# Matrix product with bias and residual: eight late residuals, another order of the first loads, a last store in more pieces

## The chip, the cores and the metric

The kernel runs on one core of a Trainium2 chip. The metric is the device time of one execution in microseconds (us), as the median of several runs. A core has five engines that run beside each other and meet only at semaphores: TensorE (PE in the profile; PEld is its loading of weights), VectorE (DVE), ScalarE (ACT), GpSimd (POOL) and SyncE (SP), which here only issues transfers. Transfers between the chip's main memory (HBM) and the on-chip memory run on 16 DMA engines. TensorE writes to PSUM, a small memory with 128 partitions, from which DVE reads here.

## The reference

```python
"x": np.random.randn(16, 512, 1024)         # float32
"weight": np.random.randn(1024, 768)
"bias": np.random.randn(768)
"residual": np.random.randn(16, 512, 768)

def reference(x, weight, bias, residual):
    return (np.matmul(x, weight) + bias + residual).astype(np.float32)
```

Flattened, x is 8192 rows of 1024, and the output and the residual are 8192 rows of 768. The kernel reads 33.6 MB of x, 25.2 MB of residual and 3.1 MB of weights, and writes 25.2 MB.

## The kernel before

**Tiles.** A tile is 128 rows of x. There are 64 tiles, in 8 super tiles of 8 (S = 0 to 7, so super tile 7 holds tiles 56 to 63). A transfer moves some of the tiles of one super tile: 4 KB per tile and partition for x, 3 KB for the residual and the output. In the table of transfers (`ORDER`), `('x', 1, 0, 4)` loads x of super tile 1, tiles 0 to 3 of it; `r` is the residual, `s` a store of the output, `w` a quarter of the weights, `b` the bias, and `c` a store of one column piece of the very last tile.

**A tile's way.** `cast` (L146, or halved L143 and L144) turns a tile of x into bf16. `transp` has TensorE transpose it, two bf16 values at a time as one 32-bit word (L154), and DVE copies the result to the chip's memory (L155). `mm` makes 16 matmuls (L161): four blocks of 256 in K, two halves of each, and 512 and 256 columns. The products of three tiles have room in PSUM (`PO`), the transposes of two (`PT`).

**Residual and bias.** For most tiles POOL adds the bias to the residual in place beforehand (L186), and DVE adds the product to that (L196); the result stands where the residual was and is stored from there. The first `EARLY_END` tiles go another way, since their residual lands late: DVE adds the product and the bias into a free buffer (L192; the buffer of residual 3, not yet loaded), and POOL adds that to the residual when it has come (L182). The residual of super tile 3 can be loaded only when all of these adds are done, and super tile 0 can be stored only then.

**Order of POOL's adds.** `pool_adds(upto)` goes through the list `ADDS` in its order, over tiles up to `upto`, and stops at the first one that can't be issued yet: its residual's load must have been issued, and for an early tile the DVE add too. It is called twice for each tile.

**Order of the transfers.** All transfers are issued by SP in the order of `ORDER`. `pump` issues, in the program's text, each one whose conditions are met: x into one of two buffers when the casts of its last user are written down, a residual into one of four buffers when the store from it is, a store when its tiles' sums are. At run time SP waits at each transfer until the instructions it depends on are done, and everything behind it in the list waits too. The weights' first landing place is the buffer of residual 1 (`w_st = R[1]`): piece S of the weights lies in its tiles 2S and 2S+1, and residual 1 can be loaded into a tile once the weight there has been cast. A transfer may name cuts of its partitions (`*cut`, `edges`), and is then issued in as many pieces.

**Head and tail.** `HEAD_ORDER` writes out the first tiles by hand: casts, transposes, weight casts (`wc`, L226), and matmuls of tiles 0 to 2 by quarters of K as the weights land. Then a loop runs over tiles 3 to 63: cast of tile t+2, POOL adds, transposes of t+1, matmuls of t, DVE's finish of t-1. The last tile's product is made in two column pieces, 512 and 256 (L255), each with its own DVE add (L259) and its own store.

Of the kernel before, what the change touches and what calls it, by code (L numbers as in the profile page):

```python
# [16 lines left out]
HEAD = 3  # L17
XT_N = 4
XB_N = 4
WARM = 12  # L20
EARLY_END = 6
TMP_SLOT = {0: 3}
ADDS = [6, 0, 7, 8, 1, 9, 2, 10, 3, 11, 4, 12, 5, 13, 14, 15]
HEAD_ORDER = [('cast', 0, 'v'), ('cast', 1, 's'), ('tr', 0), ('tr', 1), ('wc', 0, 0, 's'), ('wc', 0, 1, 'g'),
# [5 lines left out]
ORDER = [('x', 0, 0, 2), ('w', 0, 0, 2), ('x', 0, 2, 4), ('w', 1, 0, 2), ('b', 0, 0, 0), ('w', 2, 0, 2),  # L30
# [6 lines left out]


@with_exitstack
def kernel(  # L40
# [8 lines left out]
    nc = tc.nc  # L49
# [4 lines left out]
    N = weight.shape[1]  # L54
# [3 lines left out]
    chunks = [(0, 512), (512, N - 512)]  # L58
# [9 lines left out]
    def fixed(pool, name, n, shape, dt):  # L68
        return [pool.tile(shape, dt, name=f"{name}", tag=f"{name}{i}", bufs=1) for i in range(n)]
# [4 lines left out]
    XT = fixed(sb, "xt", XT_N, [P, n_q, P, 2], BF16)  # L74
    PO = fixed(ps, "psum_o", HEAD, [P, N], FP32)
# [7 lines left out]
    K_ = tc.keep_in_program_order  # L83
# [5 lines left out]
    def pump():  # L89
        while queue:  # L90
            kind, S, j0, j1, *cut = queue[0]
            if kind == "c":
                need = [("outc", j1)]
            elif kind in ("w", "b"):
                need = []
            elif kind == "x":
                need = [("cast", J * (S - X_SLOTS) + j) for j in range(j0, j1)] if S >= X_SLOTS else []
            elif kind == "r":
                need = [("store", S - RO_SLOTS, j) for j in range(j0, j1)] if S >= RO_SLOTS else []
                if S == 1:  # L100
                    need = [("wcast", n_q - 1)]
                if S in TMP_SLOT.values():
                    need = [("add", t) for t in range(EARLY_END) if TMP_SLOT[t // J] == S]
            else:
                need = [("out", J * S + j) for j in range(j0, j1)]
            if not all(n in done for n in need):
                return
            queue.pop(0)
            if kind == "b":
                K_(nc.sync.dma_start(  # L110
                    out=bias_row.rearrange("(g p) n -> g p n", p=QUAD)[:, 0, :],
                    in_=bias[None, :].to_broadcast([P // QUAD, N]),
                ))
                continue
            if kind == "w":
                K_(nc.sync.dma_start(out=w_st[:, 2 * S + j0:2 * S + j1, :], in_=w_d[:, S, j0:j1, :]))  # L116
                continue
            if kind == "x":
                K_(nc.sync.dma_start(out=X[S % X_SLOTS][:, j0:j1, :], in_=x_d[S, :, j0:j1, :]))  # L119
            elif kind == "r":  # L120
                K_(nc.sync.dma_start(out=R[S % RO_SLOTS][:, j0:j1, :], in_=res_d[S, :, j0:j1, :]))
            else:
                n0, nl = (0, N) if kind == "s" else chunks[j1]
                j1 = j1 if kind == "s" else j0 + 1
                edges = [0, *cut, P]
                for p0, p1 in zip(edges, edges[1:]):
                    K_(nc.sync.dma_start(
                        out=out_d[S, p0:p1, j0:j1, n0:n0 + nl],
                        in_=R[S % RO_SLOTS][p0:p1, j0:j1, n0:n0 + nl],
                    ))  # L130
                done.update(("store", S, j) for j in range(j0, j1))
            done.update((kind, J * S + j) for j in range(j0, j1))

    def mark(*what):
        done.add(what)
        pump()
# [30 lines left out]
    def row(t, n0=0, nl=N):  # L167
        return R[t // J % RO_SLOTS][:, t % J, n0:n0 + nl]

    def tmp(t):  # L170
        return R[TMP_SLOT[t // J]][:, t % J, :]

    adds = list(ADDS) + list(range(max(ADDS) + 1, n_t))

    def pool_adds(upto):
        for t in [t for t in adds if t <= upto]:
            if ("r", t) not in done or (t < EARLY_END and ("fin", t) not in done):
                return
            adds.remove(t)
            r = row(t)  # L180
            if t < EARLY_END:
                K_(nc.gpsimd.tensor_add(out=r, in0=r, in1=tmp(t)))  # L182
# [6 lines left out]
    def finish(t):  # L189
        p = PO[t % HEAD]  # L190
        if t < EARLY_END:
            K_(nc.vector.tensor_add(out=tmp(t), in0=p, in1=bias_sb))  # L192
# [14 lines left out]
    def bias_rows():  # L207
        K_(nc.vector.stream_shuffle(out=bias_sb, in_=bias_row, mask=[0] * QUAD))

    pump()  # L210
    for kind, *a in HEAD_ORDER:
        if kind == "bias":
# [10 lines left out]
        elif kind == "wc":  # L223
            q, e, eng = a
# [4 lines left out]
        else:  # L229
            for e in range(2):  # L230
                for n0, nl in chunks:
                    mm(a[0], n0, nl, a[1], e)
    pump()
    for t in range(HEAD - 1):
        if ("fin", t) not in done:
# [12 lines left out]
        finish(t - 1)  # L248
        pool_adds(t + 1)
    t = n_t - 1  # L250
    tail = [(PO[t % HEAD], 0, 512), (PO[(t - 2) % HEAD], 512, N - 512)]
    for p, n0, nl in tail:
        for q in range(n_q):
            for e in range(2):
                K_(nc.tensor.matmul(  # L255
                    p[:, 0:nl], lhsT=XT[t % XT_N][:, q, :, e], rhs=w_sb[:, q, e, n0:n0 + nl],
                    start=(q == 0 and e == 0), stop=(q == n_q - 1 and e == 1),
                ))
        K_(nc.vector.tensor_add(out=row(t, n0, nl), in0=p[:, 0:nl], in1=row(t, n0, nl)))  # L259
        mark("outc", chunks.index((n0, nl)))  # L260
    mark("out", t)
    pump()
    assert not queue, queue
# [30 lines left out]
```

## Time and profile before

| | us |
|---|---|
| median of 4 runs | 211.41 (211.18 to 211.48) |
| the profiled execution | 211.47, span 209.7 |
| TensorE busy | 201.4 (96%) |
| POOL busy | 116.0 (55%) |
| DVE busy | 104.7 (50%) |
| ACT busy | 67.7 (32%) |
| DMA, mean rate over the span | 416 GB/s, 87.24 MB |

The span goes from the first to the last instruction of the profiled execution; the rest of its time lies around it. A line of a group or of a timeline names the line of the code, the engine, the operation, and output<-input by the program's names; the number in square brackets is the idle time of the engine just ahead, with what ended it. SPq is SP's queue. In a row of slices the span is cut into 40 equal parts, and a digit is the busy share in tenths. In a table by stage, each row gives the stretch and its length, then the busy time and the number of instructions of PE, PEld, DVE, ACT and POOL, the granted clock of TensorE as a share, the busy share of the 16 DMA engines (a little over 1 can come out of rounding of packets), and GB/s.

A transfer over 128 partitions is split over the 16 DMA engines, and each engine reports to a semaphore when its part has landed. The transfer counts as landed at the last report.

### The profile page before, as it was taken

The page shows a single profiled execution, that of the slowest core. Times are in us where ns is not written, and L with a number is a line of the kernel's source. Part 1 is how long each engine was busy: PE and PEld are TensorE (multiplying, and loading weights), DVE is VectorE, ACT ScalarE, POOL GpSimd, SP SyncE. Part 2 cuts the span into 40 slices and gives each one's busy share as a digit, 9 for nine tenths or more (in the row PEclk, how much of TensorE's full clock was granted, in tenths as well). Part 3 has the DMA queues.
Part 4 walks back from the last instruction along what each step waited for, and adds up shares of the span by engine and source line. Part 5 has one row for each costly group of instructions (what it writes and reads, how often), then busy time and mean ns, then how long its engine had stood idle before and what let it go on. Part 6 is the DMA issues. An engine that isn't in the chain of part 4 may idle for free.

```text
span 209.7 us, 3094 instructions
## 1 busy us (share of the span) xinstructions
PE 201.4 (96%) x1273; PEld 130.2 (62%) x1298; DVE 104.7 (50%) x140; ACT 67.7 (32%) x69; POOL 116.0 (55%) x72
## 2 busy tenths in 40 slices
PE   7999997999999999999999999999999999999992
PEld 2455655666666666666666666666666666666661
DVE  0457552565375455445544554554455445445542
ACT  2444307061733053323423152330533133321000
POOL 2100089996278980199599702994069900997000
PEclk9999999999999999999999999999999999999998
DMA  6999999999999999999999999999999999999785
GB/s 235 425 428 431 427 412 439 468 406 406 455 449 408 417 436 420 431 463 391 444 431 444 425 413 427 441 428 433 436 427 439 425 417 431 444 431 419 331 379 231
DMA packets 5350, 87.24 MB, mean 416 GB/s; under 512 B 596, under 2 KB 724, under 8 KB 1496
## 3 DMA queue, kind: packets, MB, share of 16 engines
q1 hardware_dynamic: 5336, 87.05, 97.6%
q8 instruction: 10, 0.16, 0.3%
q14 instruction: 4, 0.03, 0.0%
HBM read 61.88 MB, written 25.17 MB: 415 GB/s over the span
## 4 chain that ended last, share of the span: by engine, by line
PE 82%; DMA 14%; issue 1%; ACT 1%; SPq 0%; DVE 0%; ACTq 0%
PE psum_o L161 69%; DMA x_tile<-in_x_dram 14%; PE pt L154 12%; PE psum_o L255 1%; ACT xb L146 1%; DVE ro L259 0%; SPq L116 0%; SPq L119 0%; ACTq L146 0%
## 5 line engine op out<-in xcount | busy, mean ns | idle before, releaser
L161 PE MATMUL psum_o<-w_sb,xt 128*128 128x256 bf16 (+1 forms) x983 | 172.7, 324 | 1.6 <-DVE xt L155 0.3
L161 PEld LDWEIGHTS <-xt 128*128 128x128 bf16 x1008 | 98.5, 98 | 59.0 <-DVE xt L155 0.7
L186 POOL TENSOR_TENSOR ro<-ro,bias_sb 128x768 f32<-128x768 f32 x58 | 103.3, 1820 | 51.8 <-DMA ro<-in_residual_dram 51.8
L146 ACT CAST xb<-x_tile 128x1024 bf16<-128x1024 f32 x60 | 61.2, 1044 | 114.1 <-PE pt L154 58.6
L155 DVE COPY xt<-pt 128x1024 bf16<-128x1024 bf16 x64 | 44.0, 690 | 78.1 <-PE pt L154 78.1
L196 DVE TENSOR_TENSOR ro<-psum_o,ro 128x768 f32<-128x768 f32 x57 | 54.1, 950 | 12.9 <-POOL ro L186 11.8
L154 PE MATMUL pt<-ident,xb 128*128 128x128 f32 x256 | 38.6, 275 | 1.6 <-ACT xb L146 1.4
L154 PEld LDWEIGHTS pt<-ident,xb 128*128 128x128 f32 x256 | 29.9, 142 | 10.9 <-ACT xb L146 2.1
L182 POOL TENSOR_TENSOR ro<-ro 128x768 f32<-128x768 f32 x6 | 10.7, 1810 | 18.5 <-DMA ro<-in_residual_dram 18.5
L205 PE MATMUL psum_o<-warm 128*128 128x512 bf16 x12 | 5.3, 632 | 1.2 <-DVE warm_a L201 1.2
L192 DVE TENSOR_TENSOR ro<-psum_o,bias_sb 128x768 f32<-128x768 f32 x6 | 5.6, 948 | 0.0
L226 ACT CAST w_sb<-ro 128x768 bf16<-128x768 f32 x4 | 3.3, 832 | 3.7 <-DMA ro<-in_weight_dram 3.7
L205 PEld LDWEIGHTS <-warm 128*128 128x128 bf16 x12 | 1.6, 144 | 3.9 <-issue 2.8
L226 POOL CAST w_sb<-ro 128x768 bf16<-128x768 f32 x1 | 0.8, 822 | 5.5 <-DMA ro<-in_weight_dram 5.5
L146 DVE CAST xb<-x_tile 128x1024 bf16<-128x1024 f32 x1 | 0.7, 695 | 4.5 <-DMA x_tile<-in_x_dram 4.5
L143 ACT CAST xb<-x_tile 128x512 bf16<-128x512 f32 x3 | 1.8, 616 | 3.4 <-PE psum_o L161 1.7
L255 PE MATMUL psum_o<-w_sb,xt 128*128 128x512 bf16 (+1 forms) x16 | 2.8, 326 | 0.0
L226 DVE CAST w_sb<-ro 128x768 bf16<-128x768 f32 x3 | 1.7, 558 | 2.0 <-DMA ro<-in_weight_dram 2.0
L144 DVE CAST xb<-x_tile 128x512 bf16<-128x512 f32 x3 | 1.2, 425 | 2.4 <-DMA x_tile<-in_x_dram 2.4
L255 PEld LDWEIGHTS <-xt 128*128 128x128 bf16 x16 | 1.6, 98 | 1.1
L220 PE MATMUL psum_o<-warm 128*128 128x512 bf16 x6 | 1.6, 379 | 0.0
L259 DVE TENSOR_TENSOR ro<-psum_o,ro 128x512 f32<-128x512 f32 (+1 forms) x2 | 1.1, 558 | 0.9 <-PE psum_o L255 0.8
(14 smaller groups left out, 5.0 us busy)
## 6 DMA issues: line engine op xcount, KB each, us to landing
x_tile<-in_x_dram SPq DMA_DIRECT2D x6, 4096.0 KB, 29.8
out_dram<-ro SPq DMA_DIRECT2D x7, 3072.0 KB, 28.2
ro<-in_residual_dram SPq DMA_DIRECT2D x6, 3072.0 KB, 20.7
x_tile<-in_x_dram SPq DMA_DIRECT2D x4, 1024.0 KB, 11.0
x_tile<-in_x_dram SPq DMA_DIRECT2D x2, 2048.0 KB, 25.3
ro<-in_residual_dram SPq DMA_DIRECT2D x2, 1920.0 KB, 19.2
ro<-in_weight_dram SPq DMA_DIRECT2D x4, 768.0 KB, 10.0
ro<-in_residual_dram SPq DMA_DIRECT2D x2, 1152.0 KB, 27.9
```

The source lines that it names most:

```text
L143: K_(nc.scalar.copy(out=dst[:, 0:K // 2], in_=src[:, 0:K // 2]))
L146: K_((nc.scalar.copy if how == "s" else nc.vector.tensor_copy)(out=dst, in_=src))
L154: K_(nc.tensor.transpose(out=pt[:, q, :], in_=words[:, ts(q, P)], identity=ident))
L155: K_(nc.vector.tensor_copy(out=XT[t % XT_N].rearrange("p q m e -> p (q m e)"), in_=pt.rearrange("p q m -> p (q m)").bitcast(BF16),))
L161: K_(nc.tensor.matmul(PO[t % HEAD][:, n0:n0 + nl], lhsT=XT[t % XT_N][:, q, :, e], rhs=w_sb[:, q, e, n0:n0 + nl], start=(q == 0 and e == 0) ...
L182: K_(nc.gpsimd.tensor_add(out=r, in0=r, in1=tmp(t)))
L186: K_(nc.gpsimd.tensor_add(out=r, in0=r, in1=bias_sb))
L192: K_(nc.vector.tensor_add(out=tmp(t), in0=p, in1=bias_sb))
L196: K_(nc.vector.tensor_add(out=row(t), in0=p, in1=row(t)))
L205: K_(nc.tensor.matmul(PO[0][:, 0:512], lhsT=warm[:, 0:P], rhs=warm, start=True, stop=True))
L226: K_(copy(out=w_sb[:, q, e, :], in_=w_st[:, 2 * q + e, :]))
L255: K_(nc.tensor.matmul(p[:, 0:nl], lhsT=XT[t % XT_N][:, q, :, e], rhs=w_sb[:, q, e, n0:n0 + nl], start=(q == 0 and e == 0), stop=(q == n_q ...
```

## The change

`EARLY_END` goes from 6 to 8, so that all of super tile 0 takes the way of the late residual. `ADDS` has another order. In `ORDER`, two tiles of residual 1 come before x tiles 6 and 7; residual 0 is loaded in 4 and 4 tiles and no longer in 5 and 3, with x of super tile 1 in pieces of 1 and 3 tiles between them; residual 1 follows in 4 and 2. Super tile 7 is stored in five pieces and the two column pieces: tile 59 first, cut at partition 108 into two, then 56 to 58, 60 and 61, 62. The column pieces get a list of their own (`LAST`); with its values the two pieces, their columns and their places in PSUM are what they were.

```diff
-EARLY_END = 6
+EARLY_END = 8
 TMP_SLOT = {0: 3}
-ADDS = [6, 0, 7, 8, 1, 9, 2, 10, 3, 11, 4, 12, 5, 13, 14, 15]
+ADDS = [10, 8, 11, 2, 6, 3, 13, 1, 5, 15, 7, 9, 4, 14, 0, 12]
...
 ORDER = [('x', 0, 0, 2), ('w', 0, 0, 2), ('x', 0, 2, 4), ('w', 1, 0, 2), ('b', 0, 0, 0), ('w', 2, 0, 2),
- ('w', 3, 0, 2), ('x', 0, 4, 6), ('x', 0, 6, 8), ('r', 0, 0, 5), ('x', 1, 0, 4), ('r', 0, 5, 8),
- ('r', 1, 0, 5), ('x', 1, 4, 8), ('x', 2, 0, 8), ('r', 1, 5, 8), ('r', 2, 0, 8), ('x', 3, 0, 8),
- ('s', 0, 0, 8), ('r', 3, 0, 8), ('x', 4, 0, 8), ('r', 4, 0, 8), ('s', 1, 0, 8), ('x', 5, 0, 8),
- ('r', 5, 0, 8), ('s', 2, 0, 8), ('x', 6, 0, 8), ('r', 6, 0, 8), ('s', 3, 0, 8), ('x', 7, 0, 8),
- ('r', 7, 0, 8), ('s', 4, 0, 8), ('s', 5, 0, 8), ('s', 6, 0, 8), ('s', 7, 0, 5), ('s', 7, 5, 7),
- ('c', 7, 7, 0), ('c', 7, 7, 1)]
+ ('w', 3, 0, 2), ('x', 0, 4, 6), ('r', 1, 0, 2), ('x', 0, 6, 8), ('r', 0, 0, 4), ('x', 1, 0, 1),
+ ('x', 1, 1, 4), ('r', 0, 4, 8), ('x', 1, 4, 8), ('r', 1, 2, 6), ('x', 2, 0, 8), ('r', 1, 6, 8),
+ ('r', 2, 0, 8), ('x', 3, 0, 8), ('s', 0, 0, 8), ('r', 3, 0, 8), ('x', 4, 0, 8), ('r', 4, 0, 8),
+ ('s', 1, 0, 8), ('x', 5, 0, 8), ('r', 5, 0, 8), ('s', 2, 0, 8), ('x', 6, 0, 8), ('r', 6, 0, 8),
+ ('s', 3, 0, 8), ('x', 7, 0, 8), ('r', 7, 0, 8), ('s', 4, 0, 8), ('s', 5, 0, 8), ('s', 6, 0, 8),
+ ('s', 7, 3, 4, 108), ('s', 7, 0, 3), ('s', 7, 4, 6), ('s', 7, 6, 7), ('c', 7, 7, 0),
+ ('c', 7, 7, 1)]
+LAST = [(0, 512), (512, 256)]
...
-                n0, nl = (0, N) if kind == "s" else chunks[j1]
+                n0, nl = (0, N) if kind == "s" else LAST[j1]
...
-    tail = [(PO[t % HEAD], 0, 512), (PO[(t - 2) % HEAD], 512, N - 512)]
-    for p, n0, nl in tail:
+    for i, (n0, nl) in enumerate(LAST):
+        p = PO[(t - 2 * (i % 2)) % HEAD][:, 512 * (i // 2):512 * (i // 2) + nl]
...
-        K_(nc.vector.tensor_add(out=row(t, n0, nl), in0=p[:, 0:nl], in1=row(t, n0, nl)))
-        mark("outc", chunks.index((n0, nl)))
+        K_(nc.vector.tensor_add(out=row(t, n0, nl), in0=p, in1=row(t, n0, nl)))
+        mark("outc", i)
```

More of the change, by code (lines that the diff above doesn't have):

```diff
@@ L255 @@
                 K_(nc.tensor.matmul(
-                    p[:, 0:nl], lhsT=XT[t % XT_N][:, q, :, e], rhs=w_sb[:, q, e, n0:n0 + nl],
+                    p, lhsT=XT[t % XT_N][:, q, :, e], rhs=w_sb[:, q, e, n0:n0 + nl],
                     start=(q == 0 and e == 0), stop=(q == n_q - 1 and e == 1),
                 ))
-        K_(nc.vector.tensor_add(out=row(t, n0, nl), in0=p[:, 0:nl], in1=row(t, n0, nl)))
-        mark("outc", chunks.index((n0, nl)))
+        K_(nc.vector.tensor_add(out=row(t, n0, nl), in0=p, in1=row(t, n0, nl)))
+        mark("outc", i)
     mark("out", t)
```

## The prediction

> **What bounds the kernel now.** I read the page first for who is busy, then the chain, then stretches of time, then the issues at the end.
>
> ```profile
> span 209.7 us, 3094 instructions
> PE 201.4 (96%) x1273; PEld 130.2 (62%) x1298; DVE 104.7 (50%) x140; ACT 67.7 (32%) x69; POOL 116.0 (55%) x72
> ...
> DMA  6999999999999999999999999999999999999785
> ...
> q8 instruction: 10, 0.16, 0.3%
> ```
>
> Two resources are full at once: TensorE, and the DMA engines in every slice until the last three. The third line is ten instruction loads, which matter below.
>
> The chain says what TensorE waited for, in order of time (start, length, what):
>
> ```profile
> 1.64 8.30 DMA x_tile<-in_x_dram
> 9.96 21.64 DMA x_tile<-in_x_dram
> 31.69 1.05 ACT xb L146
> 32.79 0.66 PE pt L154 x4
> ```
>
> The timeline of TensorE gives the price of that wait:
>
> ```profile
> 32.79 0.66 PE L154 MATMUL pt<-ident,xb 128*128 128x128 f32 x4 [1.39 <-ACT xb L146]
> ```
>
> Tile 8's transposes start 1.39 us late, because the first half of x of super tile 1 landed at 31.6. After that TensorE never stops: eight tiles take 24.3 us, to its end at 205.81. So the largest thing the head can give back is 1.39 us. Whether that reaches the end is seen in a table by stage (stretch, length, engines, clock, DMA share, GB/s):
>
> ```profile
> 31.50:189.00 157.50, 155.16 (x1009) 102.99 (x1030) 80.26 (x103) 56.57 (x56) 105.69 (x61) 1.00 1.01 431
> 189.00:194.00 5.00, 4.95 (x33) 3.20 (x33) 2.61 (x4) 0.59 (x1) 3.50 (x2) 1.00 0.98 419
> 194.00:199.20 5.20, 5.15 (x35) 3.44 (x35) 3.11 (x4) 0.00 (x0) 0.00 (x0) 1.00 0.79 334
> 199.20:204.40 5.20, 5.20 (x33) 3.15 (x32) 2.51 (x3) 0.00 (x0) 0.00 (x0) 1.00 0.89 379
> 204.40:209.70 5.30, 1.40 (x11) 0.81 (x9) 1.12 (x2) 0.00 (x0) 0.00 (x0) 0.87 0.59 231
> ```
>
> The DMA engines are full to 194, and some are idle around 199. The stores of the last super tile are issued at
>
> ```profile
> 199.19 0.33 SPq L127 DMA_DIRECT2D out_dram<-ro  x1
> ```
>
> ```profile
> 204.29 0.33 SPq L127 DMA_DIRECT2D out_dram<-ro  x1
> ```
>
> and at 205.75 and 206.29 (the two column pieces). The mean hides the point. The trace has, for each transfer, the sixteen moments at which its engines report. For the store of super tile 6 these are 197.35 to 199.63 on fourteen engines, but 201.18 and 201.40 on two. From there the slowest engine never rests: 201.40, then 205.96, 207.80, 208.41 and 208.72 for the four pieces of super tile 7, each as far apart as its bytes need (a full store costs an engine 194.16 to 201.40 = 7.24 us, or 0.113 us for each of its 64 rows of 3 KB). 208.72 is the last landing; the span ends 0.95 later. The other engines land the last piece at 208.42 to 208.60, behind TensorE. So the end is held twice: by two late DMA engines and, 0.12 to 0.3 us behind them, by TensorE and the last issues. Shortening one alone gives next to nothing.
>
> Why are two engines late? An engine that fetches 16 KB of instructions falls back by about 1.6 us: at 23.57 one engine is interrupted, and in the next transfer fifteen report by 25.11 and one at 26.70. The ten fetches go round eight engines: packets of one engine follow each other within 3 to 4 ns, and followed back in that way the ninth (178.68) is on the engine of the first, the tenth (197.55) on that of the second (41.71). These two are the late ones at the end. The 1.39 us stall is the same first engine's: x of super tile 1 was complete on fifteen engines at 30.00, on that one at 31.59.
>
> **Part 1, the order of loads in the head.** Two residual tiles of super tile 1 move ahead of x tiles 6 and 7; residual 0 is cut 4+4 for 5+3; x of super tile 1 is cut 1+3+4 for 4+4, with its first tile right behind the first piece of residual 0. By reports, a residual tile costs an engine 0.92 us (20.51 to 25.11 for five) and an x tile 1.22 (26.70 to 31.59 for four). From 18.10, where x tiles 4 and 5 land as before: two residual tiles 19.94; x 6 and 7 22.42; residual 0 to 3 26.10, on the interrupted engine 27.69; x tile 8 28.91; x 9 to 11 32.57; residual 4 to 7 36.25; x 12 to 15 41.1; residual 10 to 13 44.8; x of super tile 2 54.5 (before: 53.59, one residual tile less ahead); residual 14 and 15 56.35. A cast takes 1.04. With TensorE 1.39 earlier, tile 8 has to be in by 30.35, tile 9 by 33.6, tile 12 by 42.7, tile 16 by 55.0 (from the chain's transposes at 36.05, 45.16 and 57.44). All are in time, with 1.4, 1.0, 1.6 and 0.5 us to spare; tile 6 with 1.7. The stall goes: TensorE ends at 204.4. What would be late next is tile 16, at half a microsecond.
>
> SP's queue: a transfer is issued no sooner than the report of the eighth before it (issues at 7.46, 9.96, 11.85 stand on landings at 7.44, 9.94, 11.83). The residual piece now in front of x 6 and 7 also waits for the casts of the first weights, to 8.32; so x 6 and 7 are issued near 8.7, not 5.9. The engines have queued work until 18.1, which hides it. Five more issues in all, at 0.33 us each, on a queue that is mostly waiting: nothing, as long as the queue of transfers stays 17 us and more deep; uncovered they are 1.65.
>
> **Part 2, eight late residuals.** Tiles 6 and 7 change from bias on POOL and one DVE add to bias on DVE and a POOL add: 1.81 for 1.81 and 0.95 for 0.95, nothing by itself. What changes is the wait:
>
> ```profile
> 26.84 7.12 POOL L182 TENSOR_TENSOR ro<-ro 128x768 f32<-128x768 f32 x4 [18.53 <-DMA ro<-in_residual_dram]
> 34.45 1.81 POOL L186 TENSOR_TENSOR ro<-ro,bias_sb 128x768 f32<-128x768 f32 x1 [0.48 <-DMA ro<-in_residual_dram]
> ```
>
> ```profile
> 36.29 0.96 DVE L196 TENSOR_TENSOR ro<-psum_o,ro 128x768 f32<-128x768 f32 x1 [2.12 <-POOL ro L186]
> ```
>
> DVE no longer waits for POOL at tiles 6 and 7. Read against the rule that the list of adds stops at the first that isn't ready, POOL's order becomes 0, 1, 2, 3, 8, 6, 5, 7, 9, 4, 10, 11 and on. At 1.78 each from 27.69: add 8 ends at 36.6, 9 at 43.7, 4 at 45.5, 10 at 47.2. DVE's finish of tile 9 waits to 43.7 and of tile 10 to 47.2, with the copy of transposed tile 13 behind it, done at 48.8; TensorE wants that copy at 50.4. Spare 1.6 us: hidden, and beyond 1.6 each microsecond of lateness is one of TensorE. SP's store of super tile 0 and residual 3 wait for add 4 (45.5), earlier than their issue before (48.33). Nothing.
>
> **Part 3, the end.** Tile 59 is stored first, as 108 and 20 partitions, then tiles 56 to 58, 60 and 61, 62, and the column pieces. The first of these issues at the finish of tile 59, some 3 us sooner against TensorE, so the idle of 199 fills. At the end only 0.92 us of transfer (one tile) lies between the last full finish and the columns, for 1.84. With TensorE 1.39 earlier the last piece issues at 204.90 and, by its 2.4 us to landing, ends by 207.3. The late engines do not care: the bytes before super tile 7 are the same and the engines full, so they reach it at 201.40 again. Their end is 201.40 plus 0.113 for each row, whatever TensorE does: 208.7 with 64 rows. All turns on how many of tile 59's 128 rows they carry; it was eight each.
>
> No row shows a transfer of 108 partitions. Bounds: none of it on the late engines, 8 × 0.113 = 0.91 us less; or all of it on four engines with the late ones among them, 32 rows, 24 × 0.113 = 2.7 us more. The nearest row is the bias load, the one transfer here that is not 128 partitions: of 4 partitions, it reported twelve times at once (3.79) and four times with its data (11.59 to 11.80), so a count that sixteen does not divide goes to a part of the engines. Followed back packet by packet, neither late engine carried a bias row. I take the lower bound, none: 201.40 + 56 × 0.113 = 207.7, with packet gaps 207.8.
>
> What a page says of it: the Trainium skill, "DMA: Bandwidth & Descriptors", section "Why a DMA increments its semaphore by 16 and not by 1", states that a transfer uses the largest count up to 16 that divides its partitions, on the lowest-numbered engines. By it, as an estimate, 108 rows go to engines 0 to 11 and 20 to engines 0 to 9: none for 12 to 15, nine for 10 and 11, eleven for the rest. The sum is then the same 0.91 less if both late engines are of the last four, and 3 × 0.113 = 0.34 more if one is of the first ten. The fetches suggest the first: the third and fourth can be traced to engines of the bias load, the first two cannot, which fits eight engines taken two apart, with the late ones 12 and 14 or 13 and 15.
>
> The row on cutting a store in two is its issue, 0.33 us on SP. The same page, "Rules for kernel authors", speaks against it: two transfers of disjoint partitions serialise on the same engines and aren't worth it. By that rule the sum is 211.4.
>
> **Sum.** The last landing goes from 208.72 to max(207.8 late engines, 207.3 TensorE and last issue, 207.2 other engines: at most 199.63 + 67 × 0.113 if three rows of tile 59 come to each) = 207.8: 0.91 less. Profiled execution: 209.7 of span and 1.77 around it are 211.47; less 0.91 is 210.56. It stands 0.06 above the median of 211.41, so 210.5.
>
> **Rivals.** No gain: the late engines keep about eight rows, for instance with the pieces dealt evenly over sixteen. For it: no row of a 108-partition transfer. Against: the bias load. 208.7 again, 211.4; the 1.39 of TensorE is then simply idle at the end.
>
> Slower: the pieces fall on a late engine with more than its share. Place: the store of tile 59; price 0.113 us a row over eight. Up to eleven rows it stays within 0.42 (3 × 0.113 = 0.34, 211.75); from twelve on (0.45) it is a loss that shows; 32 rows are 211.4 + 2.7 = 214.1. Against it: the late engines carried no bias row.
>
> TensorE alone: my reading of the late engines is wrong and the end follows TensorE, by up to 1.39: 210.0. Against: reports spaced exactly by bytes to the last one.
>
> A stall of TensorE that comes back (tile 16, or POOL's add 10) costs nothing up to 0.5 us, the gap between 207.3 and 207.8.
>
> **How the numbers follow.** About 0.2% (0.42 us) can be told from no change. Relief of both late engines 0.62 (210.5, own range 210.2 to 210.8); TensorE alone 0.10 (210.0); no gain, or a loss up to eleven rows, 0.18 (211.4 to 211.75); slower 0.10 (from 211.85). Faster 0.72, same 0.18, slower 0.10. From 210.0 to 211.5 holds the first two and most of the third; the long bound of 214.1 is left in the tenth outside.
>
> **What would show it.** Right: no 1.39 us idle at tile 8's transposes; TensorE ends near 204.4; the report of super tile 6's store still near 201.4; the last landing near 207.8, 2.5 to 3.5 us after TensorE's end. POOL runs from 27.7 to 52 without a gap; DVE waits for POOL at tiles 9 to 12. Wrong: a last landing at 208.7 with TensorE early (no relief), or TensorE idle at tile 9, 13 or 16. The prediction falls if instruction fetches hit other engines at the end.

## The result, and the profile after

The changed kernel takes 210.79 us (median; 210.56 to 211.38) for 211.31 before, timed beside it (the four executions ahead of the prediction had 211.41): the ratio is 0.9975, 95% interval 0.9970 to 0.9979, so 0.52 us were gained. The forecast was 0.9 us, 210.5 in a range of 210.0 to 211.5, with 0.72 on faster.

The page of the changed kernel answers to the first lines shown of before:

```profile
span 209.2 us, 3104 instructions
PE 201.2 (96%) x1273; PEld 130.3 (62%) x1298; DVE 104.8 (50%) x140; ACT 67.2 (32%) x69; POOL 116.0 (55%) x72
...
DMA  6999999999999999999999999999999999999994
...
q8 instruction: 10, 0.16, 0.3%
```

No compute engine does less work, and the dip of the DMA row in the last slices is gone. The chain at tile 8 (start, length, what):

```profile
28.74 0.65 PE psum_o L163 x4
29.39 0.05 issue
29.44 1.90 PE psum_o L163 x11
31.34 0.44 PE pt L156 x4
31.78 2.60 PE psum_o L163 x16
```

Tile 8's transposes follow at 31.34 with no gap; before, they stood at 32.79 behind 1.39 us of idle. TensorE ends at 204.19 for 205.80, 1.6 us sooner, and only a third of that (0.52 us) reached the end. The table by stage (stretch, length, PE, PEld, DVE, ACT, POOL, clock, DMA share, GB/s) shows where the DMA engines took up work and where TensorE left them:

```profile
31.50:189.00 157.50, 156.45 (x1017) 103.59 (x1037) 81.42 (x104) 55.64 (x55) 105.07 (x60) 1.00 1.01 431
189.00:194.00 5.00, 4.95 (x35) 3.33 (x34) 2.60 (x4) 0.00 (x0) 4.69 (x3) 1.00 0.98 423
194.00:199.20 5.20, 5.15 (x36) 3.51 (x36) 2.24 (x4) 0.00 (x0) 0.00 (x0) 1.00 0.93 390
199.20:204.40 5.20, 4.99 (x32) 2.80 (x29) 3.21 (x5) 0.00 (x0) 0.00 (x0) 1.00 0.99 412
204.40:209.70 5.30, 0.00 (x0) 0.00 (x0) 0.25 (x1) 0.00 (x0) 0.00 (x0) 0.85 0.37 143
```

From 194 to 204.4 they move 390 and 412 GB/s for 334 and 379; from TensorE's end it is 3.9 us to the last landing, for 2.9 before. The sizes of the new stores stand in the list of transfers issued at the end (count, KB each, median us to landing; none where the list could not pair them):

```profile
out_dram<-ro SPq DMA_DIRECT2D x1, 1152.0 KB, 8.4
out_dram<-ro SPq DMA_DIRECT2D x1, 768.0 KB, 5.6
out_dram<-ro SPq DMA_DIRECT2D x1, 384.0 KB, 4.5
out_dram<-ro SPq DMA_DIRECT2D x1, 324.0 KB
out_dram<-ro SPq DMA_DIRECT2D x1, 256.0 KB, 3.7
out_dram<-ro SPq DMA_DIRECT2D x1, 128.0 KB, 3.4
out_dram<-ro SPq DMA_DIRECT2D x1, 60.0 KB
```

The last piece, 128 KB, takes 3.4 us to land for 2.4 before: it now stands behind other transfers on an engine that is late, and no longer behind TensorE. Which engine that is, the reports say. The piece of 108 partitions has twelve reports with its data (198.68 to 201.21), that of 20 has ten; the two late engines (200.89 and 201.17 for the store of super tile 6) are in neither: with nine rows of the larger piece they would report near 201.9 and 202.2, and no report stands there. The Trainium skill, "DMA: Bandwidth & Descriptors", section "Why a DMA increments its semaphore by 16 and not by 1", gives these counts: the largest number up to 16 that divides the partitions. This trace agrees, twelve and ten.

The head and the adds, in the timelines of POOL and DVE (start, length, what, idle before):

```profile
27.48 7.14 POOL L184 TENSOR_TENSOR ro<-ro 128x768 f32<-128x768 f32 x4 [19.21 <-DMA ro<-in_residual_dram]
34.56 1.84 POOL L188 TENSOR_TENSOR ro<-ro,bias_sb 128x768 f32<-128x768 f32 x1
36.33 5.37 POOL L184 TENSOR_TENSOR ro<-ro 128x768 f32<-128x768 f32 x3
```

```profile
43.50 0.96 DVE L198 TENSOR_TENSOR ro<-psum_o,ro 128x768 f32<-128x768 f32 x1 [1.88 <-POOL ro L188]
44.38 0.68 DVE L157 COPY xt<-pt 128x1024 bf16<-128x1024 bf16 x1
47.05 0.96 DVE L198 TENSOR_TENSOR ro<-psum_o,ro 128x768 f32<-128x768 f32 x1 [1.99 <-POOL ro L188]
```

POOL runs 0 to 3, 8, 6, 5, 7, 9, 4 from 27.5 on without a gap, and DVE waits for it at tiles 9 and 10, at 43.5 and 47.05 (then 0.2 us at tile 11 and 1.3 us at tile 14). TensorE waits for none of that.

### The profile page after: what moved, and what is told of

Its sections match the earlier page's. It is cut to its first block, busy times and chain, and to the rows that moved or that the text cites. A ratio compares the mean times of both kernels' runs of the same rounds, so it can differ in the third digit from the quotient of the medians.

```text
span 209.2 us, 3104 instructions
## 1 busy us (share of the span) xinstructions
PE 201.2 (96%) x1273; PEld 130.3 (62%) x1298; DVE 104.8 (50%) x140; ACT 67.2 (32%) x69; POOL 116.0 (55%) x72
## 4 chain that ended last, share of the span: by engine, by line
PE 91%; DMA 4%; issue 1%; ACT 1%; DVE 1%; SPq 0%
PE psum_o L163 77%; PE pt L156 13%; DMA x_tile<-in_x_dram 4%; PE psum_o L257 1%; ACT xb L145 1%; DVE xt L157 0%; DVE ro L261 0%; SPq L118 0%; SPq L121 0%
## 5 line engine op out<-in xcount | busy, mean ns | idle before, releaser
L188 POOL TENSOR_TENSOR ro<-ro,bias_sb 128x768 f32<-128x768 f32 x56 | 99.7, 1819 | 52.4 <-DMA ro<-in_residual_dram 52.4
L198 DVE TENSOR_TENSOR ro<-psum_o,ro 128x768 f32<-128x768 f32 x55 | 52.2, 950 | 11.9 <-POOL ro L188 10.7
L184 POOL TENSOR_TENSOR ro<-ro 128x768 f32<-128x768 f32 x8 | 14.3, 1828 | 19.2 <-DMA ro<-in_residual_dram 19.2
L194 DVE TENSOR_TENSOR ro<-psum_o,bias_sb 128x768 f32<-128x768 f32 x8 | 7.5, 948 | 0.0
```

The source lines that it names most:

```text
L188: K_(nc.gpsimd.tensor_add(out=r, in0=r, in1=bias_sb))
L198: K_(nc.vector.tensor_add(out=row(t), in0=p, in1=row(t)))
```

## The experiments

The theory: the end is held by two DMA engines made late by instruction fetches, and behind them by TensorE; so neither the head nor the stores give the gain alone, and the split of tile 59 counts because of the rows it takes off those two engines. Rivals: the stall alone, the earlier stores alone, the cut as such. Each row below holds one profile's numbers (TensorE's end, the two latest reports of the store of super tile 6, the last landing, us) and the timed ratio to the kernel before with its interval.

| kernel | TensorE ends | two latest | last landing | ratio |
|---|---|---|---|---|
| before | 205.80 | 201.18, 201.40 | 208.72 | 1 |
| changed | 204.19 | 200.89, 201.17 | 208.11 | 0.9975 (0.9970 to 0.9979) |
| changed, again | 204.43 | 201.32, 202.15 | 208.60 | 0.9974 (0.9962 to 0.9985) |
| tile 59 uncut | 204.26 | 201.19, 201.21 | 208.59 | 1.0025 (1.0016 to 1.0033) |
| head only | 204.35 | 201.10, 201.17 | 208.47 | 0.9995 (0.9986 to 1.0004) |
| tail only | 205.76 | 201.34, 201.36 | 208.13 | 0.9986 (0.9978 to 0.9995) |
| cut at 112 | 204.25 | 200.96, 201.13 | 208.52 | 1.0024 (1.0015 to 1.0033) |
| cut at 104 | 204.33 | 201.44, 201.54 | 207.95 | 0.9969 (0.9958 to 0.9980) |
| x tiles 8 to 11 whole | 206.52 | 201.28, 201.40 | 208.90 | 1.0072 (1.0045 to 1.0100) |
| six early tiles | 206.85 | 200.93, 201.22 | 209.22 | 1.0033 (1.0024 to 1.0043) |
| half of the matmuls | 191.7 | 200.09, 200.20 | 207.58 | 0.9957 (0.9938 to 0.9975) |
| three pieces | 204.38 | 201.15, 201.26 | 208.26 | 1.0008 (0.9993 to 1.0023) |
| tile 62 cut | 204.41 | 201.39, 201.52 | 207.94 | 0.9975 (0.9965 to 0.9985) |
| merged, uncut | 204.21 | 201.64, 201.95 | 209.29 | 1.0012 (1.0003 to 1.0022) |

### One half at a time

**The new head with the old stores.**

```diff
- ('s', 7, 3, 4, 108), ('s', 7, 0, 3), ('s', 7, 4, 6), ('s', 7, 6, 7),
+ ('s', 7, 0, 5), ('s', 7, 5, 7),
```

> The new head, adds and early tiles with the old stores of super tile 7 (56 to 60, then 61 and 62, then the columns). Late engines: TensorE ends near 204.3, but the last landing stays at 208.5 to 208.7; time 211.2, at most 0.1 under before. Head: 210.8. Earlier stores: 211.3, as before.

The time is 0.9995 of before, no change that can be told. Its profile by stage has the idle back in the DMA engines, with TensorE done:

```profile
194.00:199.20 5.20, 5.20 (x37) 3.42 (x34) 2.24 (x4) 0.00 (x0) 0.00 (x0) 1.00 0.91 387
199.20:204.40 5.20, 5.14 (x32) 2.94 (x30) 3.21 (x5) 0.00 (x0) 0.00 (x0) 1.00 0.90 380
204.40:209.70 5.30, 0.00 (x0) 0.00 (x0) 0.41 (x1) 0.00 (x0) 0.00 (x0) 0.98 0.46 177
```

Fourteen engines report the last piece by 207.39, the two late ones at 208.43 and 208.47: 201.17 and 7.30 for 64 rows. The 1.5 us that TensorE ends sooner are idle time at the end. The rival of the stall alone falls.

**The old head with the new stores.**

```diff
-EARLY_END = 8
+EARLY_END = 6
...
-ADDS = [10, 8, 11, 2, 6, 3, 13, 1, 5, 15, 7, 9, 4, 14, 0, 12]
+ADDS = [6, 0, 7, 8, 1, 9, 2, 10, 3, 11, 4, 12, 5, 13, 14, 15]
...
- ('w', 3, 0, 2), ('x', 0, 4, 6), ('r', 1, 0, 2), ('x', 0, 6, 8), ('r', 0, 0, 4), ('x', 1, 0, 1),
- ('x', 1, 1, 4), ('r', 0, 4, 8), ('x', 1, 4, 8), ('r', 1, 2, 6), ('x', 2, 0, 8), ('r', 1, 6, 8),
+ ('w', 3, 0, 2), ('x', 0, 4, 6), ('x', 0, 6, 8), ('r', 0, 0, 5), ('x', 1, 0, 4), ('r', 0, 5, 8),
+ ('r', 1, 0, 5), ('x', 1, 4, 8), ('x', 2, 0, 8), ('r', 1, 5, 8),
```

> The old head, adds and six early tiles with the new stores. Late engines: they end at 201.40 + 6.4 = 207.8, and then TensorE and the last issue hold the end as before the change, with the last piece landing at 208.4 to 208.6: 0.1 to 0.3 under before, 211.0 to 211.2. Head: 211.3, as before. Earlier stores: the whole 0.5, 210.8.

Here 0.3 us are gained (0.9986), as expected of the late engines; the 0.5 us of the earlier stores are not reached. The last piece lands on all sixteen engines between 207.93 and 208.13: no engine stands behind the others, so now TensorE and the last issues hold the end, a little earlier than expected because one tile, for two, is in transfer ahead of the columns.

### The cut

**Tile 59 whole.**

```diff
- ('s', 7, 3, 4, 108)
+ ('s', 7, 3, 4)
```

> The changed kernel with tile 59 stored whole, over 128 partitions. Theory of the late engines (two DMA engines, behind by instruction fetches, hold the end, and only the rows they carry matter): they take their 8 rows of tile 59 again and end at 201.17 + 7.3 = 208.5 for 207.6; the last landing is 208.5 for 208.11, time 211.2. Theory of the head (the 1.39 us stall that went is the whole gain): as the changed kernel, 210.8. Theory of the earlier stores (what counts is that super tile 7 is stored sooner and in smaller pieces): 210.8.

**Tile 59 cut evenly.**

```diff
- ('s', 7, 3, 4, 108)
+ ('s', 7, 3, 4, 112)
```

> The changed kernel with tile 59 cut at partition 112 for 108: 112 and 16 partitions, both multiples of 16, so both pieces should be dealt evenly over the sixteen engines and every engine carries eight rows again. Late engines: sixteen engines report for both pieces, the last landing is 208.5, time 211.2, as with the tile uncut. If it is the cut as such that helps (two pieces, wherever they fall): 210.8.

Both lose the whole gain and more: 1.0025 and 1.0024. In both profiles the two late engines carry their eight rows again and land last, at 208.56 and 208.59, and 208.32 and 208.52. So it isn't the cut as such, nor the earlier and smaller stores. What the theory doesn't give is the size: 208.5 to 208.6 is 0.4 to 0.5 after the changed kernel, and the timed difference is 0.5% of 211, 1.1 us. The profiled executions are among the fastest of their kernels (tile 59 whole: 211.59 of 211.49 to 212.27; cut at 112: 211.37 of 211.37 to 212.38), so what made the others longer stands in no profile. The late engines are not equally late each time: two other profiles have the later one at 202.15 (changed, again) and 201.95 (merged). Whether that is what makes the others longer isn't shown.

**Cut at 104.**

```diff
- ('s', 7, 3, 4, 108)
+ ('s', 7, 3, 4, 104)
```

> Tile 59 cut at partition 104 for 108. If a transfer takes the largest number of engines up to 16 that divides its partitions, lowest first, then 104 partitions go to thirteen engines (8 rows each) and 24 to twelve (2 each): the twelve first carry 10 rows, the thirteenth 8, the last three none. If the late engines are the fourteenth and sixteenth, they are spared and the end is the slow writer's, 10 rows for 11: 208.0, 0.1 under the changed kernel. If they are the thirteenth and fifteenth, one of them carries its 8 rows and ends near 208.5 as with the uncut tile: slower than the changed kernel by 0.4 to 1.1. If the engine numbers don't matter: as the changed kernel.

Thirteen engines report for the larger piece, twelve for the smaller, and the late ones (201.44 and 201.54) are in neither. So, if the engines are taken lowest first as the expectation has it, both are among the last three of sixteen, and the cut at 104 does as well as that at 108: 0.9969 and 0.9974 beside each other, the same within their intervals. The last landing is 207.95: the engine that lands last in the changed kernel, with 11 rows of tile 59, has 10 here, and it and the two late engines land the last piece within 0.11 us of each other (207.84 to 207.95).

**Three pieces.**

```diff
- ('s', 7, 3, 4, 108)
+ ('s', 7, 3, 4, 91, 126)
```

> Tile 59 cut at partitions 91 and 126: 91 partitions go to thirteen engines (7 rows each), 35 to seven (5 each), 2 to two (1 each), if the rule of the largest divisor holds: 13 rows on the first two engines, 12 on the next five, 7 on the eighth to thirteenth, none on the last three. If the slow writer, which ends the changed kernel with 11 rows, is the eighth, ninth or tenth, it ends at 200.0 + 63 x 0.119 = 207.5, and the last landing is the late engines' 207.6 to 207.9: 0.1 to 0.4 under the changed kernel. If it is one of the first seven, with 12 or 13 rows it ends at 208.1 to 208.2: as the changed kernel or 0.1 over.

The counts are thirteen, seven and two as the rule says. The engine that ends last carries 12 rows of tile 59 on top of 56 (eight of each of the seven other tiles), reports at 201.00 for the first piece and about 201.6 for the second, so it is one of the first seven; the first two, which carry 13 rows, report again at 199.64 and 200.09, so it is the third to the seventh. It ends at 208.26, which is 200.16 + 68 × 0.119. In the profile that is the second case of the expectation, 0.15 us after the changed kernel. The time misses it: 1.0008 is 0.7 us over the changed kernel, though the late engines carry none of tile 59, and the profiled execution, 211.13, is again among the fastest (211.03 to 212.47). Why isn't shown.

**Another place for the cut.** Tiles 56 to 59 in one piece, and tile 62 cut, or nothing cut:

```diff
- ('s', 7, 3, 4, 108), ('s', 7, 0, 3), ('s', 7, 4, 6), ('s', 7, 6, 7),
+ ('s', 7, 0, 4), ('s', 7, 4, 6), ('s', 7, 6, 7, 104),
```

> A try at a better end: tiles 56 to 59 stored in one piece, 60 and 61 in one, and tile 62, not 59, cut at partition 104 (thirteen engines with 8 rows, twelve with 2). The two late engines are spared the same eight rows, so they end at 201.2 + 6.4 = 207.6; the slow writer with 10 rows at 208.0; the last issue has 0.2 us more of transfer ahead of it, 206.7. Time as with the cut at 104 on tile 59, 0.997 of before, or up to 0.1% less if the small first pieces cost something of their own.

0.9975, no better than the changed kernel: between these two places of the cut, tile 59 and tile 62, no difference shows.

```diff
- ('s', 7, 3, 4, 108), ('s', 7, 0, 3), ('s', 7, 4, 6), ('s', 7, 6, 7),
+ ('s', 7, 0, 4), ('s', 7, 4, 6), ('s', 7, 6, 7),
```

> The same without the cut: tiles 56 to 59, 60 and 61, 62, each over 128 partitions. With tile 59 alone and uncut the time was 1.0025 of before, with the old two stores 0.9995, though the late engines land the last piece within 0.12 us of each other in the two profiles. If the small piece ahead (tile 59 alone, 3 KB rows) costs the difference: 0.9995 here. If it is the early issue of the first store: 1.0025. Late engines in the profile: 201.2 + 7.3 = 208.5.

1.0012 (1.0003 to 1.0022) lies between the two cases, and its interval holds neither 0.9995 nor 1.0025: inconclusive. Its profile caught one late engine 0.75 us later than usual, 201.95, and the last landing at 209.29.

### Why two engines are late

From tile 3 to 62, the second half of each of the four K blocks is left out, and tile 59 is uncut. The main part of the edit:

```diff
             for q in range(n_q):
-                for e in range(2):
-                    for n0, nl in chunks:
-                        mm(t, n0, nl, q, e)
+                for n0, nl in chunks:
+                    mm(t, n0, nl, q, 0, True)
```

> Are the two late engines made late by instruction fetches, or are they slow by themselves? The changed kernel with tile 59 uncut, and from tile 3 to 62 the second of each pair of matmul blocks (half of K) left out, so half of that part of the product is missing; all transfers are the same. TensorE's instructions fall from some 2570 to some 1600, its 16 KB fetches from ten to about six, so none reaches an engine a second time. If fetches make the engines late: no pair stands apart in the reports of the store of super tile 6 (before: two engines 1.5 us behind the fourteen others); the slowest is then an engine with one fetch or the slow writer, at most 0.6 us behind the next; TensorE no longer sets the pace. If the two engines are slow by themselves: the pair is there again, 1.5 us behind.

The page:

```profile
PE 139.1 (67%) x803; PEld 88.1 (42%) x818; DVE 104.8 (50%) x140; ACT 66.0 (32%) x69; POOL 115.8 (56%) x72
...
DMA  6999999999999999999999999999999999999994
...
q8 instruction: 6, 0.10, 0.2%
```

TensorE is at 67%, the DMA row as full as ever. Six 16 KB fetches are left of ten, and the pair is gone: the last four reports of the store of super tile 6 are 199.68, 200.03, 200.09 and 200.20, with no step of 1.5 us. The kernel before has the steps at the right times too: in its stores of super tiles 4 and 5 one engine stands apart (186.91 behind 185.24, 194.16 behind 192.49), after the ninth fetch at 178.68, and a second one only in the store of super tile 6, after the tenth at 197.55. So it was the second fetch on the same engine. The last landing is 207.58 with nothing cut, 15.9 us after TensorE's end, so transfers alone set the time: 0.9957, from four executions with an interval of 0.9938 to 0.9975. The changed kernel is 0.4 us above it, at the edge of that interval.

### The head

**x tiles 8 to 11 in one piece.**

```diff
-('x', 1, 0, 1), ('x', 1, 1, 4),
+('x', 1, 0, 4),
```

> The changed kernel with tiles 8 to 11 of x loaded in one piece again (for 1 and 3). They land at 32.4, the cast of tile 8 ends at 33.4, and TensorE, which wants tile 8 at 31.2, stops for 2.2 us; it ends at 206.4, the last piece is issued at 206.9 and lands 1.7 to 2.4 later, 208.6 to 209.3: slower than the changed kernel by 0.5 to 1.2. If the DMA engines alone hold the end, TensorE's stall costs nothing: as the changed kernel.

The timeline of TensorE has the stall in its place and size:

```profile
33.65 0.66 PE L155 MATMUL pt<-ident,xb 128*128 128x128 f32 x4 [2.22 <-ACT xb L147]
```

TensorE ends at 206.52, and all sixteen engines land the last piece within 0.22 us, up to 208.90: TensorE holds the end. The profiled execution is 211.87, as expected; four of the six took 213.2 to 213.7, so the ratio is 1.0072, about 2 us over the changed kernel, and the further 1.6 us are not in the profile. The record has a sign of them: the two shorter executions have a mean granted clock of 1.000, the four longer ones 0.992, and 0.8% of 210 us is 1.7 us. What lowered the clock isn't shown.

**Six early tiles, old order of adds.**

```diff
-EARLY_END = 8
+EARLY_END = 6
...
-ADDS = [10, 8, 11, 2, 6, 3, 13, 1, 5, 15, 7, 9, 4, 14, 0, 12]
+ADDS = [6, 0, 7, 8, 1, 9, 2, 10, 3, 11, 4, 12, 5, 13, 14, 15]
```

> The changed kernel with six early tiles and the old order of adds. POOL's order is 0, 1, 2, 3, 6, 4, 7, 5, 8, 9: add 6 waits for residual 4 to 7 at 36.0 and ends at 37.8, DVE's finish of tile 6 waits for it, and the copy of transposed tile 9 behind that is done at 39.4, where TensorE wants it at 37.7; with the finishes of tiles 7 and 8 TensorE loses 1.7 + 0.5 + 0.5 = 2.7 us in all. TensorE ends at 206.9, time 0.9 to 1.4 over the changed kernel. If the early tiles are worth nothing by themselves and are hidden, as my prediction costed them: as the changed kernel.

The timeline of DVE, and the waits between 28 and 62 us (total, times, longest):

```profile
37.90 0.96 DVE L198 TENSOR_TENSOR ro<-psum_o,ro 128x768 f32<-128x768 f32 x1 [5.34 <-POOL ro L188]
38.77 0.68 DVE L157 COPY xt<-pt 128x1024 bf16<-128x1024 bf16 x1
```

```profile
PE psum_o L163 <- DVE xt L157: 2.3, 3, 1.6
```

DVE stands idle 5.34 us for POOL's add of tile 6, the copy of tile 9's transposes comes at 39.45, and TensorE loses 2.3 us in three waits there, 2.5 over the run. The ratio is 1.0033, or 1.25 us over the changed kernel beside it.

**The changed kernel again**, timed beside the cut at 104, x whole and six early tiles:

> The changed kernel as it is, beside the next three: 0.9975 of the time before, as measured, if the chip makes no difference; last landing near 208.1, by an engine of the first ten.

0.9974. Here the last landing is that of a late engine, 208.60, and not of one of the first ten, whose slow one lands at 207.94: the two limits are so close that either can come last, by the execution.

## Why the prediction was right, and what was mis-sized

**The head** went as worked out. Tile 8 was cast at 28.70 (worked out 28.91), 9 to 11 from 32.39 (32.57), tile 16 from 54.51 (54.5). Tile 16's half microsecond of spare was nearly used up: other profiles of the same head have 0.2 us of idle there.

**POOL and DVE**: add 8 ended at 36.4 (36.6), DVE's finishes of tiles 9 and 10 began at 43.50 and 47.05 (43.7, 47.2). DVE's wait for POOL, named as a sign for tiles 9 to 12, was 0.2 us at 11 and none at 12. "Hidden" was right for the change as a whole. "Nothing by itself" missed what the part is for: with the new order of loads, but six early tiles and the old order of adds, TensorE waits 2.5 us for DVE's copies, so this part is worth 1.25 us as a condition of the other.

**The two holders of the end** were right: the head alone gives nothing (0.9995), the stores alone 0.3 us, together 0.52. The late engines carried none of tile 59 and landed last at 207.62, against 207.8. By the row of the bias load this was a guess among bounds, and by that row alone it was luck that it came true; the counts of reports and the cut at 104 now show it. "TensorE alone" and "no gain" are out.

**The term that was mis-sized** is the third of the maximum: "207.2 other engines: at most 199.63 + 67 × 0.113". One engine, of the first ten, writes slower than the rest: its 24 KB packets of a store take 935 to 972 ns, where the others mostly take 912. It does so in eight packets one behind the other in every full store, and in no load. In the kernel before it is one of the two engines that reported at 199.54 and 199.63. In the changed kernel it reported at 200.14, carried 67 rows at 0.119 and landed last, 208.11, half a microsecond behind the late engines. So in the profile 0.61 us were gained for 0.91. With the 0.119 us a row that this engine needs, the sum would have been 207.5 to 207.6, still below the late engines; the other half microsecond is the later start. It is there from the first full store on, where this engine's packets begin at 71.41 for 70.86 before, so it comes out of the head; its cause isn't shown.

**The rule against the cut** (the Trainium skill, "DMA: Bandwidth & Descriptors", section "Rules for kernel authors": two transfers to disjoint partition halves aren't worth it, since both go over all sixteen engines) was read in the prediction as a rule for any two disjoint pieces. The cut at 112 is its case, each piece over all sixteen engines, and changes nothing against the uncut tile (1.0024 and 1.0025). It doesn't cover pieces whose counts leave engines out: 108 and 20, or 104 and 24, are 0.5% better than the uncut tile.

What stays open: why the kernels with tile 59 whole or cut at 112 are 1.1 us slower than the changed one by time and only half as much by profile, and slower than the kernel before, although the old stores with the same rows on the late engines are not (0.9995); why the three pieces are 0.7 us slower by time; and what lowers the clock where x tiles 8 to 11 come whole, which costs 2 us and not 0.8.

## What to carry to other kernels

Where transfers are saturated to the end, look at the sixteen reports of a transfer near the end one by one before crediting any gain on the compute side: the mean busy share hid two engines 1.5 us behind. A store can be dealt unevenly on purpose by the divisors of its partition count, but each row taken from a late engine lands on another, and its margin has to be read in the same way. And a reordered load needs its whole chain of adds and copies re-timed: a part that costs nothing can be what keeps another part's gain.

## What the runs showed of the hardware

- A 16 KB instruction fetch sets one DMA engine back by about 1.6 us (26.70 for 25.11 in the next transfer). TensorE's fetches go round eight engines: followed back packet by packet in the kernel before, the ninth and the tenth fell on the engines of the first and the second, and these two stand 1.5 us behind the rest. With six fetches no pair does.
- One engine wrote to HBM 3 to 7% slower than the other fifteen (935 to 972 ns a packet for 912) in the full stores of the profiles before and after, and in no load. By the three pieces it is the third to the seventh; why it is slower isn't shown.
- A transfer of 108, 20, 104, 24, 91, 35 and 2 partitions used 12, 10, 13, 12, 13, 7 and 2 engines.
